# Output projection: from weights stationary, one pair of output tiles at a time, to token tiles stationary and weights 512 columns wide

## The chip, the cores and the metric

The kernel runs on one core of a Trainium2 chip. TensorE (PE) multiplies 128 x 128 stationary tiles with a moving operand of up to 512 columns into PSUM; VectorE (DVE) and ScalarE (ACT) do the elementwise work; DMA transfers are issued from the queues of SyncE (SP), ACT and GpSimd (POOL). GpSimd's DMAs can add to what is in the destination. The metric is the device time of one execution in microseconds; lower is better.

## The reference, cut to what matters

One layer of a streaming encoder, 512 tokens of width 2048, in float32. The normed input goes through one projection to queries, keys, values and gates of three token mixers with four heads each, and to merge gates. Each mixer's result is gated, projected up to 2048, weighted by its merge gate, and summed. The last line is what the change is about.

```python
hn = rmsnorm(x, norm_g)
proj = jnp.einsum('bsd,dc->bsc', hn, w_in)
...
up = jnp.einsum('bsnw,nwd->bsnd', ys, w_up)
merged = jnp.sum(gates * up, axis=2)
return x + jnp.einsum('bsd,de->bse', merged, w_out)
```

## The kernel before

Numbers are split into a high part in the float32r format, which PE reads in one pass, and a low part, the difference. A product is three matmuls: high by high, high by low, low by high. ACT makes the high part of a weight tile (`split`, line 249), DVE the low part (line 253).

The projections use seven block products in place of eight (Strassen's scheme in Winograd's form). The blocks are the two halves of the input dimension, two weight tiles or two blocks of weight columns, and the two halves of the tokens, 256 each. On the data's side the combinations are made once. For the output projection these are `m1` (products 1 and 5), `m2` (2 and 3), `m23` (6 and 7) and `m4` (4), one for each of eight pairs of merged tiles (`merged_a`, `merged_b`, from line 1672). On the weights' side they are made for each task: w5 = a21 + a22 and w7 = a11 + a21 by DMAs of GpSimd that add onto a tile just loaded (`add_up`, line 291), w6 = w1 + w5 and w3 = w2 + w6 by DVE (`sums`, lines 658 and 664).

A `PairTask` (line 614) makes two tiles of 128 output columns for all tokens, as seven units of one product each. A unit has a weight tile of eight 128 x 128 blocks, which are stationary; the data move. For each block j, a matmul of 512 columns takes the high and low parts of the data side by side, and a matmul of 256 columns takes the low weights with the high data. The two halves of the PSUM bank are added on the way out (`fold`). Products 6, 7, 4 and 3 go on in the bank of 1, 6, 7 and 5 (`ONTO`).

The stages, in order on PE: the columns of the input projection with the three mixers' attention between them, until 1008 us; the up projection, 16 tiles of two units each; the output projection, `out_pair(e)` for eight pairs of output tiles (line 1723). Its first pair is `late`: its order is 1, 5, 2, 3, 6, 7, 4, its banks are not shared, and it uses 256-wide matmuls only, three for each block. The last product of the last pair has 256-wide matmuls too (`plain_end`). Outputs are 128 output columns on partitions by 512 tokens; x is loaded as xT and added by DVE (lines 1738, 1746 and 1753), and stores go out on ACT's queue (lines 1740, 1747 and 1755).

The order of the instructions is written by a planner when the program is built. Every stretch of work is a generator that yields an engine and a cost, an event, or slots of a buffer. `Flow.run` always takes the task that can start first, and among several the one that is due first. So the orders on PE, ACT, DVE and SP's DMAs are fixed in the program, and each engine waits only for the data of its next instruction. GpSimd has no clock in the plan. An `add_up` of a pair task is not pinned in the order, while those of the value tasks (`pinned=True`, line 945) are; the transfer time is counted at 170 KB per us behind the load, in the order in which loads are listed.

Buffers: six raw weight tiles of 512 KB (`NR`), three split ones (`LA` + 1), 20 tiles of 256 KB (`NT`), 28 split data tiles (`NX`), eight PSUM banks (two of `acc0`, one each of `acc1` and `acc2`, four of `att`). A unit is prepared from the start of the unit two places ahead of it.

`ValueTask` (line 885) is the one place that already has data stationary and weights moving: two token blocks take turns with 256 weight columns.

Of the kernel before, what the change touches and what calls it, by code (L numbers as in the profile page):

```python
# [9 lines left out]
F32R = mybir.dt.float32r  # L10
# [6 lines left out]
P = 128  # L17
HP = P // 2
S = 512
# [18 lines left out]
PE, ACT, DVE, SP = 0, 1, 2, 3  # L38
# [26 lines left out]
class Flow:  # L65
# [98 lines left out]
def hybrid_kernel(  # L164
# [126 lines left out]
    def add_up(to, src, ready, kb, pinned=False):  # L291
        i = nc.gpsimd.dma_start(to, src, accum_op=ALU.add)  # L292
# [91 lines left out]
    def load_unit(u):  # L384
        if isinstance(u, (Pair, VUnit)):
            if u is u.task.units[0]:
                yield from u.task.load()
            return
# [203 lines left out]
    class Pair(Unit):  # L592


        def __init__(self, task, i):
            super().__init__(task.mms_of(i), task.after_of(i))
            self.task, self.p = task, task.order[i]
            self.single = task.late or task.plain_end and self.p == 4
            self.onto = None if task.late else ONTO.get(self.p)
            self.turns, self.opens = not self.single, self.onto is None  # L600
# [13 lines left out]
    class PairTask:  # L614
# [9 lines left out]
        def __init__(self, src1, src2, ops, c1_done=None, c2r_done=None, c2_done=None, late=False, rest=None,  # L624
                     x1_first=False, plain_end=False):
            self.plain_end = plain_end
            self.src, self.ops, self.late, self.rest = (*src1, *src2), ops, late, rest
            self.done = {"c1": c1_done, "c2r": c2r_done, "c2": c2_done}
            self.order = (1, 5, 2, 3, 6, 7, 4) if late else (1, 2, 6, 5, 7, 3, 4)
# [4 lines left out]
            self.r, self.r_ev, self.c2_ev, self.right_ev = None, Event(), Event(), Event()  # L634
# [38 lines left out]
        def mms_of(self, i):  # L673
            p = self.order[i]
            bank = (0, 1, 2, 0, 0, 1, 2)[i] if self.late else {2: 1, 5: 2, 3: 2}.get(p, 0)
            self.bank[p] = bank

            def go(u):
                single, onto = u.single, u.onto
# [8 lines left out]
                def high(first):  # L688
                    for j in range(UK):
# [4 lines left out]
                        if single:  # L694
                            yield PE, mm_us(HS)
                            mm(self.ps[p][:, LH], u.hi[:, j, :], r[:, 0, :], start, stop, more)
                            yield PE, mm_us(HS)
                            mm(self.ps[p][:, LH], u.hi[:, j, :], r[:, 1, :], more=more)
                        else:
                            yield PE, mm_us(S)  # L700
                            mm(two(self.ps[p]), u.hi[:, j, :], r, start, stop, more)
# [16 lines left out]
        def after_of(self, i):  # L718
# [20 lines left out]
            def late():  # L739
                ps, bank = self.ps[p][:, LH], accs[self.bank[p]]  # L740
                if p == 1:
                    yield from new("u")
                    yield ACT, act_us(HS)
                    nc.scalar.activation(self.u[:, LH], ps, AF.Copy)
                elif p == 5:
                    yield from new("c2")
                    yield ACT, act_us(HS)
                    nc.scalar.activation(self.c2[:, RH], ps, AF.Copy)
                elif p == 2:
                    yield from new("c1")  # L750
                    yield ev[1]
                    yield h
                    add(self.c1[:, LH], self.u[:, LH], ps)
                elif p == 3:
                    yield ev[2]
                    yield ev[5]
                    yield h
                    add(self.c1[:, RH], self.c2[:, RH], ps)
                elif p == 6:
                    yield ev[2]  # L760
                    yield h
                    add(self.u[:, LH], self.u[:, LH], ps)
                elif p == 7:
                    yield ev[6]
                    yield h
                    add(self.u[:, RH], self.u[:, LH], ps)
                else:
                    yield ev[7]
                    yield h
                    minus(self.c2[:, LH], self.u[:, RH], ps)  # L770
                give(bank)
                set_(ev[p])
                if p == 6:
                    yield ev[3]
                    yield h
                    add(self.c1[:, RH], self.c1[:, RH], self.u[:, LH])
                    finished("c1", self.c1)
                elif p == 7:
                    yield ev[3]
                    yield h  # L780
                    minus(self.c2[:, RH], self.c2[:, RH], self.u[:, RH])
                    finished("c2r", self.c2[:, RH])
                elif p == 4:
                    give(t2s)
# [1123 lines left out]
```

## Time and profile before

| what | value |
|---|---|
| median of 3 runs | 1298.85 us (1298.83 to 1299.65) |
| the profiled execution | 1298.3 us |
| its span, first to last instruction | 1296.5 us |
| PE busy | 1289.8 us, 99% |
| DVE busy | 1148.6 us, 89% |
| ACT busy | 884.3 us, 68% |
| GpSimd busy | 106.9 us, 8% |
| first to last matmul of the output projection | 1135.6 to 1293.2 us |
| granted PE clock | 1.000 |

Times inside the span are counted from its first instruction. A row of a group reads: line, engine, operation, output <- inputs, shapes, count, then busy us and mean ns of one, then the engine's idle time ahead of these instructions and what ended it. The ends of matmuls are modelled, and a matmul's duration overlaps the next one's, so that the distance from one start to the next tells the pace. PEld stands for the loads of stationary tiles. A row of a timeline reads: start, length, engine, line, operation, tiles, shape, count.

### The profile page before, as it was taken

The numbers are of one execution on the slowest core, as the hardware profiler recorded it, in microseconds if no ns is written. First come the engines' busy times: TensorE is split into PE (matmuls) and PEld (weight loads), VectorE is DVE, ScalarE is ACT, GpSimd is POOL, SyncE is SP. The second block draws the span as 40 slices with busy tenths as digits, with TensorE's granted clock in tenths as the row PEclk, the third lists the DMA queues.
The fourth block names the chain that finished last, engine by engine and source line by source line (L and its number), as shares of the span: only waits on it lengthen the run. The fifth ranks groups of instructions, "written<-read, shape, count | busy, mean of one in ns | idle before, by whom it ended". The sixth has DMA issues, their size and how long they took to land.

```text
span 1296.5 us, 20194 instructions
## 1 busy us (share of the span) xinstructions
PE 1289.8 (99%) x7247; PEld 1127.6 (87%) x7247; DVE 1148.6 (89%) x1693; ACT 884.3 (68%) x1380; POOL 106.9 (8%) x138
## 2 busy tenths in 40 slices
PE   9999999999999999999999999999999999999998
PEld 6888888888888888888888888888888888898887
DVE  8988889888998999989799999999899888898776
ACT  8887677777767668676766785967858555454443
POOL 0200001020110000102010000100000000001000
PEclk9999999999999999999999999999999999999999
DMA  9879798888889778888897888888988755778893
GB/s 341 236 189 234 195 239 195 216 197 230 223 198 251 181 209 207 243 207 232 209 237 202 191 230 220 200 241 188 234 222 273 240 191 188 204 206 244 233 255 97
DMA packets 132420, 282.90 MB, mean 218 GB/s; under 512 B 43344, under 2 KB 51536, under 8 KB 132320
## 3 DMA queue, kind: packets, MB, share of 16 engines
q1 hardware_dynamic: 111200, 217.32, 54.0%
q0 software_dynamic: 17376, 59.78, 27.2%
q10 hardware_dynamic: 3744, 4.52, 1.0%
q8 instruction: 57, 0.93, 0.3%
q14 instruction: 43, 0.35, 0.1%
HBM read 249.92 MB, written 24.42 MB: 212 GB/s over the span
## 4 chain that ended last, share of the span: by engine, by line
PE 92%; DVE 4%; DMA 1%; issue 1%; ACT 1%; SPq 1%; DVEq 0%; ACTq 0%
PE acc L268 77%; PE att L268 10%; DVE w L253 2%; PE att L1386 1%; PE att L1387 1%; PE att L264 1%; PE att L265 1%; SPq L281 1%; PE att L263 1%; PE att L1385 1%; DVE m L253 0%; DMA tt<-p 0%; DMA lf_parts<-fd 0%; DMA gl<-c 0%; DVE c L538 0%
## 5 line engine op out<-in xcount | busy, mean ns | idle before, releaser
L253 DVE TENSOR_TENSOR w<-raw,w 128x1024 fp32r<-128x1024 f32 (+2 forms) x424 | 500.3, 1185 | 96.2 <-ACT w L249 95.4
L249 ACT ACTIVATE w<-raw 128x1024 fp32r<-128x1024 f32 (+2 forms) x424 | 434.7, 1026 | 173.1 <-PE acc L268 78.6
L268 PE MATMUL acc<-x,w 128*128 128x512 f32 (+1 forms) x2656 | 497.2, 339 | 0.7 <-ACT w L408 0.7
L268 PEld LDWEIGHTS acc<-x,w 128*128 128x128 f32 x2656 | 426.0, 189 | 66.5 <-issue 2.5
L268 PE MATMUL acc<-t,w 128*128 128x512 f32 (+1 forms) x1920 | 358.7, 338 | 0.4 <-DVE w L253 0.3
L268 PEld LDWEIGHTS acc<-t,w 128*128 128x128 f32 x1920 | 291.5, 190 | 33.3 <-ACT vh L249 0.4
L268 PE MATMUL acc<-m,w 128*128 128x256 f32 (+1 forms) x960 | 157.3, 327 | 0.3 <-DVE m L253 0.3
L268 PEld LDWEIGHTS acc<-m,w 128*128 128x128 f32 x960 | 141.4, 190 | 16.3 <-DVE m L253 0.5
L292 POOL DMA_DIRECT2D raw<-in_w_col x80 | 69.0, 863 | 776.2 <-DMA raw<-in_w_col 298.8
L268 PE MATMUL att<-y,w 128*128 128x512 f32 x384 | 89.6, 389 | 0.0
L268 PEld LDWEIGHTS att<-y,w 128*128 128x128 f32 x384 | 72.1, 188 | 14.9
L268 PE MATMUL acc<-w,x 128*128 128x512 f32 (+1 forms) x336 | 63.8, 339 | 0.0
L818 ACT ACTIVATE u<-acc 128x512 f32<-128x512 f32 x49 | 29.1, 594 | 46.5 <-PE acc L268 44.2
L797 ACT ACTIVATE u<-acc 128x512 f32<-128x512 f32 x50 | 29.7, 594 | 43.3 <-PE acc L268 35.0
L658 DVE TENSOR_TENSOR raw<-raw,raw 128x1024 f32<-128x1024 f32 x48 | 58.6, 1221 | 0.3
L664 DVE TENSOR_TENSOR raw<-raw,raw 128x1024 f32<-128x1024 f32 x48 | 58.6, 1220 | 0.2
L268 PEld LDWEIGHTS acc<-w,x 128*128 128x128 f32 x336 | 52.2, 190 | 7.1 <-issue 0.4
L538 DVE TENSOR_TENSOR c<-c,begin_in 128x512 f32<-128x512 f32 x80 | 54.3, 686 | 0.2
L852 ACT ACTIVATE c<-acc 128x256 f32<-128x256 f32 x49 | 18.7, 381 | 49.7 <-PE acc L268 41.9
L801 ACT ACTIVATE v<-acc 128x512 f32<-128x512 f32 x53 | 31.5, 594 | 28.3 <-PE acc L268 28.1
L737 DVE TENSOR_TENSOR c<-u 128x256 f32<-128x256 f32 x105 | 44.3, 425 | 3.2
L268 PE MATMUL acc<-y,w 128*128 128x512 f32 x192 | 46.1, 389 | 0.0
(216 smaller groups left out, 1359.6 us busy)
## 6 DMA issues: line engine op xcount, KB each, us to landing
raw<-in_w_col SPq DMA_DIRECT2D x200, 512.0 KB, 4.9
raw<-in_w_col POOLq DMA_DIRECT2D x80, 512.0 KB, 6.7
raw<-in_w_out SPq DMA_DIRECT2D x40, 512.0 KB, 4.3
raw<-in_w_v SPq DMA_DIRECT2D x24, 512.0 KB, 5.4
gl<-c SPq DMA_DIRECT2D x48, 256.0 KB, 3.9
raw<-in_w_up SPq DMA_DIRECT2D x32, 384.0 KB, 3.8
sg<-gl SPq DMA_DIRECT2D x48, 256.0 KB, 3.9
raw<-in_w_out POOLq DMA_DIRECT2D x16, 512.0 KB, 7.3
```

The lines of the kernel that those rows point to most:

```text
L249: nc.scalar.activation(hi, src, AF.Copy)
L253: nc.vector.tensor_sub(lo, src, f(hi))
L268: nc.tensor.matmul(ps, w, x, start=start, stop=stop, skip_group_check=more)
L292: i = nc.gpsimd.dma_start(to, src, accum_op=ALU.add)
L538: nc.vector.tensor_mul(c, c if src is None else src, rstd[0][:c.shape[0], :])
L658: nc.vector.tensor_add(w[1], w[1], w[5])
L664: nc.vector.tensor_add(w[2], w[2], w[1])
L737: add(to, src[:, LH], src[:, RH])
L797: nc.scalar.activation(self.u, ps, AF.Copy)
L801: nc.scalar.activation(self.v, ps, AF.Copy)
L818: nc.scalar.activation(self.s, ps, AF.Copy)
L852: nc.scalar.activation(c, ps[:, RH], AF.Copy, scale=-1.0)
```

## The change

The output projection is written anew. `OutTask` g (two of them) makes 1024 output columns as two blocks of 512; tokens are on partitions. A unit `OutUnit` is one product p on a quarter kq of its input dimension: two input blocks (`QK`) of 512 weight columns. For each of the two 128-token blocks s of a product, the token tile is stationary and 512 weight columns move: high by high, low data by high weights, and, once the low weights are there, high data by low weights. That is 12 matmuls of 512 in a unit, 28 units in a task. All three parts add up in the same columns, so there is no fold. The units of products 1 and 5 come first, those of 4 last; the last unit of all cuts its second token block into two halves of 256 columns.

Results go by DVE straight from PSUM onto tiles that hold x, loaded by rows of tokens from `xn` (`begin`, `result`), and the tiles are stored from SP's queue, the last half one from ACT's. Product 7's weight is w6 less a22, subtracted by DVE (`seventh`), in place of a load and an add on GpSimd; product 4's weight comes in 256 KB tiles. The split of `m4` moves from the up projection (`merged_b`) to a task that waits for the end of the up projection (`merged_d`), and it takes data tiles in place of 256 KB tiles. The late first pair, `plain_end` and what belongs to them are removed.

In the whole kernel GpSimd becomes an engine of the planner (`POOL`): an `add_up` waits in the plan until its load has landed (`added`), takes 0.8 us of GpSimd and is pinned in the order; its transfer counts at 190 KB per us. The first loads of a value task's product 7, which are issued by GpSimd too, are listed in the same way, and the extra 1 us on the value task's sums (`VLATE`) goes. The input `w_out` and the output are laid out to match.

```diff
...
-PE, ACT, DVE, SP = 0, 1, 2, 3
+PE, ACT, DVE, SP, POOL = 0, 1, 2, 3, 4
...
-    LATE = (0.3, 0.12, 0.12, 0.0)
+    LATE = (0.3, 0.12, 0.12, 0.0, 0.0)
 
     def __init__(self):
-        self.clock = [0.0] * 4
-        self.idle = [0.0] * 4
+        self.clock = [0.0] * 5
+        self.idle = [0.0] * 5
...
-    def add_up(to, src, ready, kb, pinned=False):
-        i = nc.gpsimd.dma_start(to, src, accum_op=ALU.add)
-        if pinned:
-            tc.keep_in_program_order(i)
-        line[0] = max(line[0], ready + 1.0) + kb / 170.0
+    def add_up(to, src, kb):
+        yield POOL, 0.8
+        tc.keep_in_program_order(nc.gpsimd.dma_start(to, src, accum_op=ALU.add))
+        line[0] = max(line[0], flow.fin + 1.0) + kb / 190.0
         return Event(line[0] + 2.5)
+
+    def added(there, begun, parts):
+
+        yield begun
+        for to, src, kb in parts:
+            ev = yield from add_up(to, src, kb)
+        there.t = ev.t
...
                 ev = yield from fetch(t, srcs[0], 512)
                 if len(srcs) > 1:
-                    ev = add_up(t, srcs[1], ev.t, 512)
-                self.there[p].t = ev.t
+                    spawn(added(self.there[p], ev, [(t, srcs[1], 512)]), 0.0, flow.fin)
+                else:
...
                 for to, c in pieces(p, kh):
                     w, kb = src({5: 2, 1: 0, 2: 1, 7: 0, 4: 3}[p], kh)[:, c], 128 * (c.stop - c.start)
-                    if queue is nc.sync:
+                    if p == 7:
+                        yield POOL, 0.8
+                        tc.keep_in_program_order(nc.gpsimd.dma_start(to, w))
+                        ev = Event(landing(flow.fin, kb))
+                    else:
                         ev = yield from fetch(to, w, kb)
-                    else:
-                        tc.keep_in_program_order(queue.dma_start(to, w))
-                        ev = Event(landing(flow.ready + 0.5, kb))
+                if p in (5, 7):
+                    more = [(to, src({5: 3, 7: 2}[p], kh)[:, c], 128 * (c.stop - c.start)) for to, c in pieces(p, kh)]
+                    return lambda: spawn(added(self.there[p, kh], ev, more), 0.0, flow.fin)
...
                 if p == 5:
-                    add(p, kh)
+                    add()
+            adds = []
             for kh in range(2):
-                yield from begin(7, kh, nc.gpsimd)
+                adds.append((yield from begin(7, kh)))
+            for add in adds:
+                add()
             for kh in range(2):
-                add(7, kh)
-            for kh in range(2):
-                yield from begin(4, kh, nc.sync)
+                yield from begin(4, kh)
...
-        yield t2s, 1
-        parts, ev = t2("m4", F32R), Event()
-        yield from split(parts[:, LH], parts[:, RH], b[:, RH], HS, ev)
-        give(t2s)
-        m4[k] = two(parts), parts[:, LH], ev
+        spawn(merged_d(k, b), 6.0, flow.fin)
...
-    mops = strassen_ops(m1, m2, m23, None)
-    mops[4] = lambda k: m4[k]
...
-    def out_pair(e):
...
+    mops = strassen_ops(m1, m2, m23, m4)
+
+    def merged_d(k, b):
+
+        yield up_done
+        for i in range(UK):
+            yield lambda: m23[i] is not None
+        if k % 2 == 0:
+            yield xps, 1
+            m4[k // 2] = Parts("m4")
+        yield lambda: m4[k // 2] is not None
+        h, lo, ev = m4[k // 2].half(k % 2)
+        yield from split(h, lo, b[:, RH], HS, ev, (up_done.t + 10.0 + k,))
+        give(t2s)
...
+    QK = UK // 4
...
+    class OutUnit(Unit):
+
+
+        def __init__(self, task, p, kq):
+            super().__init__(task.mms, None, (QK, S))
+            self.task, self.p, self.kq = task, p, kq
...
+        def __init__(self, g, last):
+            self.g, self.last = g, last
+            order = [(p, q) for q in range(4) for p in (1, 5)]
+            order += [(6, 0), (2, 0), (6, 1), (3, 0), (2, 1), (6, 2), (3, 1), (2, 2), (6, 3), (3, 2), (2, 3)]
+            order += [(7, q) for q in range(4)] + [(3, 3)] + [(4, q) for q in range(4)]
+            self.w, self.there = {}, {o: Event() for o in order}
+            self.units = [OutUnit(self, *o) for o in order]
...
+        def load(self):
+            def src(i, kq):
+                return w_out[self.g, i // 2, i % 2, kq]
+
+            def begin(p, kq):
+                yield raws, 1
+                t = raw_tile((QK, S))
+                self.w[p, kq] = [t]
+                ev = yield from fetch(t, src({1: 0, 5: 2, 2: 1}[p], kq), 512)
+                if p == 5:
+                    spawn(added(self.there[p, kq], ev, [(t, src(3, kq), 512)]), 0.0, flow.fin)
+                else:
+                    self.there[p, kq].t = ev.t
+
+            def pairs():
+                for kq in range(4):
+                    yield t2s, QK
+                    self.w[4, kq] = [t2("raw").rearrange("p (j c) -> p j c", j=1) for _ in range(QK)]
+                    for j, t in enumerate(self.w[4, kq]):
+                        ev = yield from fetch(t, src(3, kq)[:, j:j + 1], 256)
+                    self.there[4, kq].t = ev.t
+
+            for o in ((5, 0), (1, 0), (5, 1), (1, 1), (5, 2), (5, 3), (1, 2), (1, 3)):
+                yield from begin(*o)
+            for kq in range(4):
+                if kq == 1:
+                    spawn(pairs(), 0.5, flow.fin)
+                yield from begin(2, kq)
...
+        def sums(self):
+            n = dve_us(QK * S)
+            for kq in range(4):
+                yield self.there[1, kq]
+                yield self.there[5, kq]
+                yield self.unit(1, kq).ready
+                yield DVE, n, flow.ready + 4.0
+                a = self.w[1, kq][0]
+                nc.vector.tensor_add(a, a, self.w[5, kq][0])
+                self.w[6, kq] = [a]
+                set_(self.there[6, kq])
+                spawn(self.free(5, kq), 1.0)
+            for kq in range(4):
+                yield self.there[2, kq]
+                yield self.unit(2, kq).ready
+                yield DVE, n, flow.ready + 1.0
+                self.w[3, kq] = [a] = self.w[2, kq]
+                nc.vector.tensor_add(a, a, self.w[6, kq][0])
+                set_(self.there[3, kq])
+                spawn(self.seventh(kq), 1.0)
+
+        def seventh(self, kq):
+            yield self.unit(6, kq).ready
+            yield self.there[4, kq]
+            self.w[7, kq] = [a] = self.w[6, kq]
+            for j, t in enumerate(self.w[4, kq]):
+                yield DVE, dve_us(S), flow.ready + 6.0
+                nc.vector.tensor_sub(a[:, j:j + 1], a[:, j:j + 1], t)
+            set_(self.there[7, kq])
+
+        def free(self, p, kq):
+
+            yield self.unit(p, kq).ready
+            give(raws)
...
+        def begin(self):
+            for i in (1, 4, 2, 3):
+                for s in range(2):
+                    yield t2s, 1
+                    b, c = (s, 2 + s, s, 2 + s)[i - 1], 2 * self.g + (i > 2)
+                    t = self.o[i, s] = t2("o")
+                    self.o_ev[i, s].t = (yield from fetch(t, xn[b, c], 256)).t
...
+        def mms(self, u):
+            p, kq = u.p, u.kq
+            onto = ONTO.get(p)
+            ends = self.last and p == 4 and kq == 3
...
+            def step(s, part, cols):
+                for j in range(QK):
+                    k = kq * QK + j
+                    yield lambda: mops[p](k) is not None
+                    r, _, ev = mops[p](k)
+                    yield ev
+                    yield PE, mm_us(cols.stop - cols.start)
+                    w = u.lo if part == 1 else u.hi
+                    mm(self.ps[p, s][:, cols], r[:, part // 2, s * P:(s + 1) * P], w[:, j, cols],
+                       onto is None and kq + j + part == 0, kq == 3 and j == QK - 1 and part == 1, True)
+
+            whole = slice(0, S)
+            if ends:
+                yield u.ready
+                for s, cols in ((0, whole), (1, LH), (1, RH)):
+                    yield from bank(s)
+                    for part in (0, 2, 1):
+                        yield from step(s, part, cols)
+                    spawn(self.result(p, s, cols), 0.0, flow.fin)
+                return
+            for s in range(2):
+                yield from bank(s)
+                for part in (0, 2):
+                    yield from step(s, part, whole)
+            yield u.ready
+            for s in range(2):
+                yield from step(s, 1, whole)
+                if kq == 3:
+                    spawn(self.result(p, s, whole), 0.5, flow.fin)
+
+        def result(self, p, s, cols):
+            ps = self.ps[p, s][:, cols]
+            add, sub = nc.vector.tensor_add, nc.vector.tensor_sub
+            first = {1: (1, add), 5: (4, sub), 6: (2, add), 4: (3, sub)}.get(p)
+            then = {2: (1, add, 1), 3: (2, add, 6), 7: (4, sub, 5)}.get(p)
+            i, do = (first or then)[:2]
+            if first:
+                yield self.o_ev[i, s]
+            else:
+                yield self.ev[then[2], s]
+            o = self.o[i, s][:, cols]
+            yield DVE, dve_us(cols.stop - cols.start)
+            do(o, o, ps)
+            if p not in (1, 5, 6, 7) and cols.stop == S:
+                if s:
+                    give(atts)
+                else:
+                    give(accs[{2: 1, 3: 2, 4: 0}[p]])
+            if cols.stop == S:
+                set_(self.ev[p, s])
+            if p in (2, 3, 7, 4):
+                b, c = (s, 2 + s, s, 2 + s)[i - 1], 2 * self.g + (i > 2)
+                if cols.start:
+                    nc.scalar.dma_start(out[b, c][:, cols], o)
+                else:
+                    t2s.free.append((yield from store(out[b, c][:, cols], o, 256)))
+
+    for g in range(2):
+        units.extend(OutTask(g, g == 1).units)
...
-VLATE = 1.0
...
-_OUT = (DT, P, S)
+_OUT = (QB, NQ, P, S)
...
-        "w_out": g["w_out"][0].reshape(2, UK, P, DT, P).transpose(3, 0, 2, 1, 4),
+        "w_out": g["w_out"][0].reshape(2, 4, 2, P, 2, 2, S).transpose(4, 5, 0, 1, 3, 2, 6),
...
-    return np.ascontiguousarray(o.reshape(D, S).T).reshape(1, S, D)
+    return np.ascontiguousarray(o.reshape(QB, NQ, P, S).transpose(0, 2, 1, 3)).reshape(1, S, D)
...
```

More of the change, by code (lines that the diff above doesn't have):

```diff
@@ L597, in __init__ @@
             self.task, self.p = task, task.order[i]
-            self.single = task.late or task.plain_end and self.p == 4
-            self.onto = None if task.late else ONTO.get(self.p)
-            self.turns, self.opens = not self.single, self.onto is None
+            self.onto = ONTO.get(self.p)
+            self.turns, self.opens = True, self.onto is None
         def source_there(self):
@@ L674, in mms_of @@
             p = self.order[i]
-            bank = (0, 1, 2, 0, 0, 1, 2)[i] if self.late else {2: 1, 5: 2, 3: 2}.get(p, 0)
+            bank = {2: 1, 5: 2, 3: 2}.get(p, 0)
             self.bank[p] = bank
             def go(u):
-                single, onto = u.single, u.onto
+                onto = u.onto
                 more = onto is not None
@@ L737, in fold @@
                     add(to, src[:, LH], src[:, RH])
[L739 to L783, printed above, removed]
-                    give(t2s)
-                    finished("c2", self.c2)
-            def go():
-                if i == 0 and self.rest is not None:
-                    spawn(self.rest(self), 1.0)
-                if self.late:
-                    yield from late()
-                    return
+            def go():
                 ps, bank = self.ps[p], self.pools[self.bank[p]]
@@ L1763, in hybrid_kernel @@
-    for e in range(0, DT, 2):
-        units.extend(out_pair(e))
+    mops = strassen_ops(m1, m2, m23, m4)
[10 more added lines that the diff above has]
+        give(t2s)
```

121 lines of the change are left out of this document (48 added, 73 removed).

## The prediction

> **What bounds the kernel now.** I read the page first: the engines' shares and the chain that ended last.
>
> ```profile
> PE 1289.8 (99%) x7247; PEld 1127.6 (87%) x7247; DVE 1148.6 (89%) x1693; ACT 884.3 (68%) x1380; POOL 106.9 (8%) x138
> ...
> PE 92%; DVE 4%; DMA 1%; issue 1%; ACT 1%; SPq 1%; DVEq 0%; ACTq 0%
> ```
>
> TensorE (PE) is busy for 99% of the span and carries 92% of the chain. VectorE (DVE) is next at 89%, close enough to become the bound wherever the change loads it. Next, busy time by stretches of the span (columns: stretch, its length, then busy time and instructions of PE, weight loads, DVE, ScalarE and GpSimd, the granted clock, DMA share, GB/s):
>
> ```profile
> 0.00:300.00 300.00, 297.36 (x1648) 254.80 (x1649) 266.80 (x419) 230.71 (x410) 32.13 (x50) 1.00 0.85 226
> 300.00:600.00 300.00, 300.00 (x1729) 265.39 (x1728) 272.66 (x387) 217.92 (x330) 28.11 (x34) 1.00 0.86 217
> 600.00:900.00 300.00, 300.00 (x1732) 265.62 (x1731) 276.94 (x413) 217.13 (x333) 25.92 (x31) 1.00 0.86 216
> 900.00:1008.00 108.00, 107.57 (x621) 94.92 (x620) 97.94 (x145) 77.59 (x121) 6.91 (x8) 1.00 0.91 237
> 1138.00:1155.00 17.00, 16.68 (x139) 16.41 (x138) 16.86 (x27) 8.10 (x13) 0.87 (x1) 1.00 0.48 136
> 1155.00:1280.00 125.00, 125.00 (x723) 110.50 (x722) 99.35 (x124) 59.09 (x71) 10.36 (x12) 1.00 0.85 238
> ```
>
> The clock is full everywhere. Before 1008 us PE idles 2.64 + 0 + 0 + 0.43 = 3.1 us, so a better order can win almost nothing there, and a worse one can lose. The output projection (from 1135.6 us) is PE's too, except that in its first part DVE is busy for 16.86 of 17.00 us. What counts in that stage is how long PE's stream of matmuls takes. A matmul's own duration is modelled and overlaps the next, so I take strides: stretches divided by counts. The chain by time gives the up projection, all matmuls 512 wide; the PE timeline gives a value unit, which already holds token tiles stationary while weights move:
>
> ```profile
> 1007.91 5.44 PE att L268 x24
> ```
>
> ```profile
> 603.41 1.07 PE L268 MATMUL acc<-w,t 128*128 128x512 f32 x4
> ...
> 605.23 0.64 PE L268 MATMUL acc<-w,t 128*128 128x256 f32 x4
> ...
> 607.14 1.09 PE L268 MATMUL acc<-w,t 128*128 128x512 f32 x4
> 608.07 1.07 PE L268 MATMUL att<-w,t 128*128 128x512 f32 x4
> 608.98 0.39 PE L268 MATMUL acc<-w,x 128*128 128x512 f32 x1
> ```
>
> 24 in 5.44 us is 0.2267 us for a 512-wide matmul. In the value unit eight take 605.23 - 603.41 = 1.82 us (0.2275 each) and sixteen 256-wide ones 607.14 - 605.23 = 1.91 us (0.119). The next eight 512-wide ones take 608.98 - 607.14 = 1.84 us (0.230): long ones right after short ones are slower. Now the output projection itself, its groups by shape, then PE's busy time in two stretches:
>
> ```profile
> L268 PEld LDWEIGHTS acc<-m,w 128*128 128x128 f32 x960 | 141.4, 190 | 16.3 <-DVE m L253 0.5
> ...
> L268 PE MATMUL acc<-m,w 128*128 128x512 f32 x384 | 92.8, 391 | 0.0
> ...
> L268 PE MATMUL acc<-m,w 128*128 128x256 f32 x576 | 74.3, 283 | 0.3 <-DVE m L253 0.3
> ```
>
> ```profile
> 1135.60:1293.20 157.60, 157.26 (x961) 1.00 0.75 209
> 1160.00:1280.00 120.00, 120.00 (x691) 1.00 0.85 237
> ```
>
> Between 1160 and 1280 us the widths alternate eight by eight or sixteen by sixteen, half of each, so 691 matmuls in 120 us make 0.3473 us for one of each, and a 256-wide one costs 0.3473 - 0.2267 = 0.1206 us. At equal columns two short ones cost 2 x 0.1206 - 0.2267 = 0.0145 us more than a long one. The count closes: 384 x 0.2267 + 576 x 0.1206 = 156.5 us of the stage's 157.60; the other 1.1 us are 0.32 us of idle (the row 1138 to 1155), the drain of the last matmul and the slower long ones.
>
> **The change part by part.**
>
> *Matmuls.* Columns stay: 384 x 512 + 576 x 256 = 344,064 before, and 56 units of 12 x 512, also 344,064, after. The count falls from 960 to 672, or 678 with six of the last unit cut in two: 666 x 0.2267 + 12 x 0.1206 = 152.4 us, with 0.15 us of drain 152.6, against 157.6 us: **-5.0 us**, all on the path. The other end takes the value unit's slow stride for all: 666 x 0.230 + 1.45 + 0.15 = 154.8 us, so -2.8 us. I take -5.0, because the slow stride stands behind short matmuls, and the new stream has none before its last unit. The stationary load must stay hidden: 190 ns, one for every matmul as before, now under a stride of 227 ns instead of partly 121.
>
> The Trainium skill, "TensorE: Matmul & The Clock Gate", section "Back-to-back issue gap", speaks against this term: it gives N/2.4 + 2.5 ns for the gap, a fixed 2.5 ns per matmul, by which 282 fewer matmuls bring only 0.7 us and the stage would not pay. The rows disagree (0.2267 and 0.1206 us lie 13 to 14 ns above N/2.4), and the sum goes by the rows.
>
> *Changeover from the up projection.* Before, products 1 and 5 cover 48 x 0.1206 = 5.8 us, then product 2 needs the last merged tile. After, products 1 and 5 cover 96 x 0.2267 = 21.8 us with m1 alone. Prices on DVE (groups after 1149 us), and ScalarE's (ACT) split:
>
> ```profile
> L253 DVE TENSOR_TENSOR w<-raw,w 128x1024 fp32r<-128x1024 f32 x51 | 62.1, 1223 | 25.6 <-ACT w L249 25.6
> L664 DVE TENSOR_TENSOR raw<-raw,raw 128x1024 f32<-128x1024 f32 x7 | 8.5, 1221 | 0.0
> ...
> L822 DVE TENSOR_TENSOR v<-v,acc 128x512 f32<-128x512 f32 x7 | 4.8, 687 | 0.0
> ...
> L1746 DVE TENSOR_TENSOR c<-c,xr 128x256 f32<-128x256 f32 x8 | 3.4, 421 | 0.1
> ```
>
> ```profile
> L249 ACT ACTIVATE w<-raw 128x1024 fp32r<-128x1024 f32 x49 | 51.7, 1056 | 32.4 <-PE acc L268 16.9 <-DVE c L1746 3.4 <-DVE w L253 3.0
> ```
>
> DVE in one group of 28 units: 28 low parts x 1.22 = 34.2 us, 8 weight sums x 1.22 = 9.8, 8 subtractions for product 7 x 0.69 = 5.5, 14 results x 0.69 = 9.7. That is 59.2 us beside 336 x 0.2267 = 76.2 us of PE, or 78% (before: 99.35 of 125, 79%). The folds, ACT's copies out of PSUM and the separate additions of x go; they lay beside PE, so nothing is gained. But the first group also gets the rest of the merging: 8 x 0.69 for m23, 8 x 0.42 for m4 (moved here from the up projection), and some 4 us for the last tile by my estimate from the same rows. That is 72 us of 76, 95%. A unit's low part is used only after eight of its twelve matmuls, 1.8 us in, and its split is begun two units ahead, so lateness of a few us is covered. I charge +0.5 us, near the 0.32 us that PE idles today with DVE at 99%; the ends are 0 and 4 us (the room that is left).
>
> *Loads and stores.* Per group 12 plain tiles, 4 added onto and 8 halves: 10 MB, 20 MB in all, against 56 x 0.5 = 28 MB.
>
> ```profile
> raw<-in_w_out SPq DMA_DIRECT2D x40, 512.0 KB, 4.3
> ...
> raw<-in_w_out POOLq DMA_DIRECT2D x16, 512.0 KB, 7.3
> ```
>
> The tightest tile is (1, 2), the seventh for six buffers: it waits until (5, 0) is summed, and PE needs it 4 x 2.72 = 10.9 us into the stage. With 4.3 us to land and 1.06 us to split, the sum must be done 5.5 us in; I expect it by 3. If that cover goes, PE waits for the difference. Stores of results move from ACT's queue to SP's, where the tile loads behind them wait for the result too; those loads run some five units (13.6 us) ahead, which hides a late result of 0.69 us. GpSimd's 8 adds instead of 16, and 16 loads of x as before, lie beside PE as well: nothing.
>
> *The end.* The last part is subtracted and stored as before:
>
> ```profile
> 1293.23 0.42 DVE L849 TENSOR_TENSOR c<-c,acc 128x256 f32<-128x256 f32 x1 [1.00 <-PE acc L268]
> 1293.68 0.34 ACTq L1755 DMA_DIRECT2D out<-c  x1
> ```
>
> That store ends the span 2.8 us after its issue. After, 512 KB instead of 384 KB leave in the last 1.5 us; 128 KB at the 237 GB/s above are 0.5 us. I take +0.3 us between 0 and 0.5.
>
> *GpSimd (POOL) in the list.* All its DMAs get a written order and count as 0.8 us of an engine; weight sums fall due at other planned times, so the written orders of DVE and ACT shift everywhere. Is anyone waiting for adds today (columns: total us, times, longest)?
>
> ```profile
> POOL raw L292 <- DMA raw<-in_w_col: 298.8, 29, 16.4
> ...
> ACT w L249 <- DMA raw<-in_w_col: 1.7, 1, 1.7
> ```
>
> POOL waits 298.8 us for the loads that it adds to, while ACT waits for such tiles once, 1.7 us: they lie ready early, which covers the order of the adds. I take 0. The ends are -1 us (the 0.43 us of idle from 900 us on, and as much from the 2.64) and +8.5 us, below.
>
> **Sum.** -5.0 + 0.5 + 0.3 + 0 = -4.2 us. The profiled execution took 1298.3 us, so 1294.1; the median of the runs, 1298.85, lies 0.55 us above it, so 1294.6 us.
>
> **The rivals.**
>
> *DVE holds the first group.* At 95% the written order breaks somewhere, for instance at (1, 2): 3 to 4 us of PE idle in place of 0.5, so 1294.6 + 3 = 1297.6 us, no change. For it: DVE at 16.86 of 17.00 today. Against: that stretch loses only 0.32 us, and products 1 and 5 now cover four times as much.
>
> *Fewer matmuls don't pay.* Then the change doesn't do what it says: with each long matmul behind a new stationary tile at 157.6 / 672 = 0.2345 us the time is as before, 1298.9 us. For it: the 0.230 above points that way. Against: 0.2275 in the same unit, each matmul there with another token tile. The Trainium skill's gap, named above, would put the time there too; no row bears it out.
>
> *A written POOL order stalls PE upstream (slower).* An add queued behind one whose tile is late comes late by one landing, 7.3 us in the row above; with a lead of two units (16 x 0.3473 = 5.6 us) PE loses 1.7 us each time. Three such places eat the gain, five among the 40 column pairs make 1294.6 + 8.5 = 1303.1 us. For it: PE has no idle to give between 300 and 900 us, and DVE stands at 272.66 and 276.94 of 300 in an order written anew. Against: ACT hardly waits for tiles.
>
> *The new order also closes gaps.* The changeover costs nothing and 1 us goes upstream: 1294.6 - 0.5 - 1 = 1293.1 us.
>
> **How the numbers follow.** Forecast 0.58, closed gaps 0.10, DVE in the first group 0.12, fewer matmuls for nothing 0.05, POOL 0.15. About 0.2% (2.6 us) is what a measurement can tell from no change, so the bounds are 1296.25 and 1301.45 us: faster 0.58 + 0.10 = 0.68, same 0.12 + 0.05 = 0.17, slower 0.15. The range leaves out the POOL rival: from 1291.3 (closed gaps, an end that costs nothing and 1.5 us more upstream) to 1299.5 us (matmuls for nothing, 0.6 us of stall beside them). The forecast alone, with its bounds, spans 1293.5 to 1297.
>
> **What would show it.** PE's timeline of the output projection should have 678 matmuls in about 153 us, nearly all 512 wide, 227 ns apart. A stage of 158 us without idle says matmuls for nothing; idle behind w or raw in its first 76 us says DVE or loads; PE idle well above 3.1 us before 1008 us says the written order. The prediction is wrong if the long stride is not 227 ns there, or if PE gains over 2 us of idle anywhere.

## The result and the profile after

The changed kernel takes 1296.26 us (median of 14 runs, 1294.24 to 1299.18) against 1299.5 us (14 runs, 1297.39 to 1300.3): 3.2 us less, a ratio of 0.9978 with a 95% interval of 0.9971 to 0.9986. The profiled execution took 1295.77 us, its span 1294.0. From its page, the engines' shares and the chain:

```profile
PE 1286.2 (99%) x6965; PEld 1112.3 (86%) x6965; DVE 1137.9 (88%) x1666; ACT 873.4 (68%) x1359; POOL 100.0 (8%) x130
...
PE 93%; DVE 3%; DMA 2%; ACT 1%; SPq 1%; issue 1%; ACTq 0%; DVEq 0%
```

PE still carries the time, with 282 matmuls fewer. Now the same stretches as in the prediction (busy time of PE, weight loads, DVE, ScalarE and GpSimd, then clock, DMA share and GB/s), and the output projection's matmuls by shape with PE's busy time from its first matmul to its last:

```profile
0.00:300.00 300.00, 298.01 (x1652) 255.26 (x1653) 266.39 (x420) 233.44 (x413) 32.22 (x50) 1.00 0.84 225
300.00:600.00 300.00, 300.00 (x1731) 265.29 (x1730) 272.58 (x388) 219.11 (x332) 29.88 (x36) 1.00 0.86 219
600.00:900.00 300.00, 298.67 (x1722) 264.06 (x1721) 274.16 (x409) 212.94 (x325) 24.11 (x28) 1.00 0.84 214
900.00:1008.00 108.00, 107.40 (x618) 94.24 (x617) 98.95 (x146) 77.14 (x120) 6.90 (x8) 1.00 0.90 236
1138.00:1155.00 17.00, 17.00 (x77) 14.08 (x76) 16.93 (x26) 11.14 (x18) 0.00 (x0) 1.00 0.56 186
1155.00:1280.00 125.00, 125.00 (x553) 103.47 (x552) 98.01 (x111) 49.27 (x53) 3.45 (x4) 1.00 0.52 159
```

```profile
L268 PE MATMUL acc<-w,m 128*128 128x512 f32 x336 | 94.2, 389 | 0.0
L268 PE MATMUL att<-w,m 128*128 128x512 f32 x330 | 92.6, 389 | 0.0
L268 PE MATMUL att<-w,m 128*128 128x256 f32 x12 | 1.9, 290 | 0.5 <-DVE o L1846 0.5
```

```profile
1137.30:1290.60 153.30, 152.78 (x679) 1.00 0.50 156
1160.00:1280.00 120.00, 120.00 (x531) 1.00 0.50 153
```

Three things are to be seen. The stage has 678 matmuls, 226 ns apart (120 us for 531), and lasts 153.4 us instead of 157.6. It begins at 1137.3 us instead of 1135.6, mostly because PE stood for 1.3 us between 600 and 900 us, where it stood for nothing before. And near the end PE waits once, 0.5 us, for DVE. The spans differ by 2.5 us: -4.2 from the stage and +1.7 ahead of it, while what follows the last matmul is as long as before (3.3 us).

The loss upstream, on ACT and on PE, and the wait near the end:

```profile
657.99 0.63 ACT L249 ACTIVATE vh<-vr 128x512 fp32r<-128x512 f32 x1 [3.38 <-DMA vr<-vd]
658.53 0.58 ACT L742 ACTIVATE u<-acc 128x512 f32<-128x512 f32 x1
659.16 1.20 PE L268 MATMUL acc<-t,w 128*128 128x512 f32 x4 [1.33 <-ACT u L742]
```

```profile
1289.54 0.42 DVE L1846 TENSOR_TENSOR o<-o,att 128x256 f32<-128x256 f32 x1 [0.38 <-PE att L268]
1290.02 0.62 PE L268 MATMUL att<-w,m 128*128 128x256 f32 x3 [0.52 <-DVE o L1846]
```

ACT stands 3.38 us for `vr`, the value tiles read back from DRAM for a head's attention. Behind it stands the copy `u`, which frees the PSUM bank in which PE's next product goes on. Near the end, PE writes the right half of a bank only when DVE has read its left half.

### The profile page after: what moved, and what is told of

It reads as the page before. It is cut to its first block, busy times and chain, and to the rows that moved or that the text cites. A ratio compares the mean times of both kernels' runs of the same rounds, so it can differ in the third digit from the quotient of the medians.

```text
span 1294.0 us, 19495 instructions
## 1 busy us (share of the span) xinstructions
PE 1286.2 (99%) x6965; PEld 1112.3 (86%) x6965; DVE 1137.9 (88%) x1666; ACT 873.4 (68%) x1359; POOL 100.0 (8%) x130
## 4 chain that ended last, share of the span: by engine, by line
PE 93%; DVE 3%; DMA 2%; ACT 1%; SPq 1%; issue 1%; ACTq 0%; DVEq 0%
PE acc L268 72%; PE att L268 17%; DVE w L253 1%; SPq L281 1%; DMA vr<-vd 1%; PE att L264 1%; PE att L265 1%; PE att L263 1%; PE att L1321 1%; PE att L1322 1%; PE att L1320 0%; DMA lf_parts<-fd 0%; ACT w L249 0%; DMA tt<-p 0%; DMA raw<-in_w_one 0%
## 5 line engine op out<-in xcount | busy, mean ns | idle before, releaser
L268 PE MATMUL att<-w,m 128*128 128x512 f32 (+1 forms) x342 | 94.5, 386 | 0.5 <-DVE o L1846 0.5
L268 PE MATMUL acc<-w,m 128*128 128x512 f32 x336 | 94.2, 389 | 0.0
L268 PEld LDWEIGHTS att<-w,m 128*128 128x128 f32 x342 | 63.6, 188 | 13.7 <-DVE o L1846 0.7
L268 PEld LDWEIGHTS acc<-w,m 128*128 128x128 f32 x336 | 63.1, 188 | 13.2
L662 DVE TENSOR_TENSOR raw<-raw,raw 128x1024 f32<-128x1024 f32 x40 | 48.8, 1220 | 0.4
L668 DVE TENSOR_TENSOR raw<-raw,raw 128x1024 f32<-128x1024 f32 x40 | 48.7, 1218 | 0.2
L742 ACT ACTIVATE u<-acc 128x512 f32<-128x512 f32 x43 | 25.5, 594 | 33.4 <-PE acc L268 33.2
L1548 ACT ACTIVATE sg<-sg,small_in 128x512 f32<-128x512 f32 x48 | 33.4, 715 | 21.4 <-DMA sg<-gl 21.4
L763 ACT ACTIVATE u<-acc 128x512 f32<-128x512 f32 x42 | 24.9, 592 | 33.0 <-PE acc L268 30.7
```

Of the source, the lines that this page charges most:

```text
L268: nc.tensor.matmul(ps, w, x, start=start, stop=stop, skip_group_check=more)
L662: nc.vector.tensor_add(w[1], w[1], w[5])
L668: nc.vector.tensor_add(w[2], w[2], w[1])
L742: nc.scalar.activation(self.u, ps, AF.Copy)
L763: nc.scalar.activation(self.s, ps, AF.Copy)
L1548: nc.scalar.activation(g, g, AF.Sigmoid, bias=bg[:, n * DT + d:n * DT + d + 1])
```

## The experiments

My theory was the prediction's: the count of matmuls carries the gain, and the changeover, the end and the list of GpSimd's queue cost what was put down. The rivals were that the list stalls PE, that DVE binds the changeover, and that the count is not what pays. Below, what PE "lost" at a place is the distance from one matmul's start to the next, less the usual stride; that is about 0.16 us more than the wait that a row shows. Ratios are to the kernel before as it ran beside each experiment.

**The two parts apart.** First the new output projection without the list:

```diff
-    def add_up(to, src, kb):
-        yield POOL, 0.8
-        tc.keep_in_program_order(nc.gpsimd.dma_start(to, src, accum_op=ALU.add))
-        line[0] = max(line[0], flow.fin + 1.0) + kb / 190.0
+    def add_up(to, src, ready, kb, pinned=False):
+        i = nc.gpsimd.dma_start(to, src, accum_op=ALU.add)
...
+        line[0] = max(line[0], ready + 1.0) + kb / 170.0
```

> The new output projection alone; GpSimd's adds are as in the kernel before (not in the plan, counted at 170 KB per us behind their load). Theory: the gain is the projection's stream of matmuls and the list costs about 1.5 us upstream (GpSimd listed, weight loads are planned closer together, the reload of the value tiles, vr from vd, lands late, and ACT with the copy that frees a PSUM bank stands behind it). Then the projection starts near 1135.6 us as before, lasts 153 to 153.5 us, ACT waits for vr by under 1 us in total, and the time is 4.2 us under the kernel before, ratio 0.9968. Rival: the stall upstream comes from any replanning, the list is innocent: start near 1137 and ratio 0.998 as the changed kernel.

Measured: 1297.75 us against 1299.18, ratio 0.9990 (0.9982 to 0.9999). The projection starts at 1136.0 us, so less is lost upstream, but it lasts 155.7 us: PE loses 2.26 us in the changeover. ACT's waits for `vr` are 3.2 us in three places, where the theory had under 1. PE's waits, the largest (total, times, longest):

```profile
PE acc L268 <- DVE w L253: 2.8, 3, 2.1
```

Neither theory had this. Then the list alone, by the same lines put into the kernel before:

> The kernel before with GpSimd in the plan alone, the old output projection. Theory: ACT's waits for vr grow to some 6 us as in the changed kernel, PE stalls by 1 to 2 us before 1008 us, and the time is 1 to 1.7 us over the kernel before, ratio 1.001. Rival (list innocent): ratio 1.000 within 0.0005 and no PE wait over 0.7 us between 100 and 900 us. A third: the list gains, ratio under 0.9995.

Measured: 1299.92 us, ratio 1.0004 (0.9995 to 1.0013). ACT's waits for `vr` did grow, from 0.6 us in one place to

```profile
ACT vh L249 <- DMA vr<-vd: 7.2, 5, 2.4
```

but PE lost only 0.21 us at 658 us and started the projection at 1135.8. So the list has no price of its own that this can show. How much of the waits for `vr` it brings is not shown either: they were 3.2 us without it, above, and 2.7 to 7.5 us in six executions of the changed kernel's order (below). They reach PE only when the landing is late enough.

**The late `vr`.** One edit planned every landing of `vr` later, a second one only that of the eighth head, the one at 657 us (with the interleaved end, below):

```diff
-            yield ev
+            yield Event(ev.t + 3.0)
...
-            yield ev
+            yield Event(ev.t + (3.0 if (self.n, self.h) == (B, 3) else 0.0))
```

> The changed kernel with the landing of vr planned 3 us later, all else the same, so that ACT takes other work first. Theory (late vr is the stall at 657 us): ACT's waits for vr go from 6.9 us to under 2, PE's wait of 1.3 us for ACT's copy at 657 us goes, the time is about 1.4 us under the changed kernel (ratio to before near 0.9967) and the runs scatter less than its 5 us. Rival: the stall only moves to another place or was of that one execution: ratio 0.998 and the same scatter.

Measured: 1297.65 us, ratio 0.9993 (0.9984 to 1.0002), no faster than without the edit. ACT's waits for `vr` fell to 0.2 us and the stall at 657 us went, as the theory had it. But the whole order was planned anew, and PE now lost 1.12 us at 264 us and 1.06 us in the changeover, and the scatter stayed (1296.28 to 1300.19). The cause was right and the remedy wrong: here the stall that was planned away was replaced by others.

> As the run with the interleaved end, and one landing of vr alone, that of the eighth head (649 us), planned 3 us later, which moves its attention work behind the next product and leaves the rest of the order as it is. Theory (ACT stands at this late vr with the copy that frees PE's bank behind it): PE's stall at 657 us, 1.5 and 2.3 us in two executions of the same order, goes, nothing else moves, and the time is 1.5 to 2 us under the interleaved end alone: ratio near 0.9960, and the scatter of runs shrinks. Rival (a stall follows from the DMA load there and takes the next waiting instruction): the time is as with the interleaved end alone.

Measured: 1294.57 us, ratio 0.9969 (0.9959 to 0.9978). Only 29 places of PE's order differ from the changed kernel's, 12 of them in the last unit. PE is busy for 300.00 of 300.00 us between 600 and 900 us, and the projection starts at 1135.1. The run with the later `m4` (below) has the same order there and loses nothing at 657 us either. The place is settled by that, but the time lies within the interval of the interleaved end alone, so what it is worth on average was not shown.

**The end.** First the last unit in one piece, then its three pieces in another order:

```diff
-                for s, cols in ((0, whole), (1, LH), (1, RH)):
+                for s, cols in ((0, whole), (1, whole)):
...
+                for s, cols in ((1, LH), (0, whole), (1, RH)):
```

> The changed kernel with the second token block of the very last unit in one piece of 512 columns, not two of 256. Theory: the 0.67 us in which PE waits for DVE's read of the left half before it writes the right half of the same bank goes, and six matmuls fewer save 0.09 us; the last subtraction is 0.27 us longer (0.69 for 0.42) and the last store has 256 KB instead of 128 KB (0 to 0.4 us): 0.1 to 0.5 us faster than the changed kernel. Rival: PE's wait has another cause and stays: 0.2 to 0.6 us slower than it.

Measured: 1296.37 us, ratio 0.9982 (0.9973 to 0.9991), as the changed kernel. PE's wait near the end is gone, but what follows the last matmul grew from 3.32 to 3.93 us, so both sides cancel. Up to that unit the order is the changed kernel's, so this is also a second execution of it: at 657 us PE lost 2.34 us, with 1.6 us more behind it at a lower clock (last section), and 0.53 us in the changeover.

> The changed kernel with the last unit in another order: left half of the second token block, then the whole first block, then the right half. The order of all other work is unchanged. Theory (PE waits for DVE's read of the left half before it writes the right half of the same bank): the read hides behind the first block's 1.36 us, PE's wait of 0.5 us near the end goes, the stage from its first to its last matmul is 0.67 us shorter than the changed kernel's, and the end after it stays 3.3 us: ratio 0.0005 under that of the changed kernel. Rival: the wait stands for something else and stays.

Measured: 1295.11 us, ratio 0.9966 (0.9954 to 0.9978). DVE reads the left half while PE works on the other block, the wait is gone, and 0.2 us of it come back after the last matmul (3.52 us). Without what was lost in the changeover the stage is 0.67 us shorter, as expected. The time is not clearly under the changed kernel's: the intervals of the ratios overlap. In this third execution of the order PE lost 0.62 us at 657 us and 0.95 in the changeover.

**Is it the count?** Every long matmul of the stage was cut into two on the same stationary tile:

```diff
-                    mm(self.ps[p, s][:, cols], r[:, part // 2, s * P:(s + 1) * P], w[:, j, cols],
+                    for c in ((LH, RH) if cols == whole else (cols,)):
+                        mm(self.ps[p, s][:, c], r[:, part // 2, s * P:(s + 1) * P], w[:, j, c],
```

> The changed kernel with every 512-wide matmul of the new output projection cut into two of 256 columns onto the same stationary tile: the same columns, 1344 matmuls. Theory (a matmul costs 13 to 14 ns beside its columns, so the count carries the gain): 120 ns each, the stage grows from 153.4 to about 161.5 us, 8 us more. Rival (the cost per matmul is about 2.5 ns, and the gain came from elsewhere, such as the late first pair or fewer evictions): 672 x 2.5 ns, the stage grows by 1.7 us to about 155.

The sums come out otherwise than the reference's, perhaps because both halves that open a bank carry its start flag, which was not tested; the matmuls are all there. Measured: one run of 1306.90 us. PE's busy time in the stage:

```profile
1139.60:1301.80 162.20, 161.67 (x1345) 1.00 0.48 149
```

At equal columns 666 more matmuls cost 162.2 - 153.4 = 8.8 us, 13 ns each. Both stages hold the same 0.67 us near the end and lose nothing in the changeover. The theory holds, and the rival's 1.7 us is excluded. Each half also loads its stationary tile anew (1344 loads in the stage), so the 13 ns belong to a matmul with its load; which of the two makes them stays open. The run's order up to the projection is the changed kernel's once more: it lost 1.73 us at the late `vr`, 1.52 at 115 us, and started the projection at 1139.6 us.

**Who binds the changeover?** Eight more DVE operations of 0.69 us in the first 22 us:

```diff
+            def more():
+                yield DVE, dve_us(S), flow.ready + 0.5
+                nc.vector.tensor_add(x_begin, x_begin, x_begin)
+
+            if self.g == 0 and p in (1, 5):
+                spawn(more(), 0.5, flow.fin)
```

> The changed kernel with one more 512-wide addition on DVE (0.69 us, on a tile that nothing reads any more) in each of the first group's eight units of products 1 and 5: 5.5 us more for DVE in the first 22 us of the output projection, where it is busy for 10.63 of 10.70 and 12.00 of 12.00 us. Theory of the prediction (a few us of lateness are covered): PE loses under 1.5 us there. Rival (DVE is already the bound there, the cover is used up): PE loses 3 to 5.5 us in that stretch.

Measured: one run of 1300.99 us. PE's busy time in three stretches (the column after the count is the granted clock):

```profile
1137.00:1149.00 12.00, 12.00 (x54) 1.00 0.57 184
1149.00:1161.00 12.00, 7.61 (x29) 0.94 0.47 146
1161.00:1163.00 2.00, 2.00 (x6) 0.51 1.02 290
```

PE lost 2.42 and 2.30 us, 4.7 in all: the rival holds. Up to the second wait six of the eight additions had run, 3.6 us at their pace of 0.60 us. The runs of the same order whose projection starts as early (1135.8 and 1135.3 us, here 1135.9) lost 0.95 and 1.35 us without them, so 3.4 to 3.8 us are due to the additions: next to nothing was covered. DVE is the bound of the changeover. This is also why a stall upstream and the wait here don't simply add: in the changed kernel's profile DVE ends the low part that PE waits for at 1155.2 us and in the other two at 1154.8 to 1154.9, while PE starts the stage 1.4 to 1.9 us later in the first and so loses nothing.

What does DVE do there? Its timeline in the run with the interleaved end, up to the row for which PE waits, and PE's:

```profile
1151.49 1.22 DVE L1751 TENSOR_TENSOR raw<-raw,raw 128x1024 f32<-128x1024 f32 x1
1152.62 1.09 DVE L253 TENSOR_TENSOR m<-sg,m 128x256 fp32r<-128x256 f32 x3
1153.63 1.22 DVE L253 TENSOR_TENSOR w<-raw,w 128x1024 fp32r<-128x1024 f32 x1
```

```profile
1154.90 0.73 PE L268 MATMUL acc<-w,m 128*128 128x512 f32 x2 [0.79 <-DVE w L253]
```

The three rows of 256 columns are splits of `m4`, which no matmul reads for about another 48 us (product 4 begins 24 units, 65 us, into the stage); the low part that PE waits for stands behind them. So they were made due later, in two kernels: the one with one later `vr` and the interleaved end, and the new projection without the list.

```diff
-        yield from split(h, lo, b[:, RH], HS, ev, (up_done.t + 10.0 + k,))
+        yield from split(h, lo, b[:, RH], HS, ev, (up_done.t + 28.0 + k,))
```

> As the run with one vr later and the interleaved end, and the splits of m4, which product 4 needs only 65 us into the output projection, due 18 us later in the plan; all before the projection keeps its order. In the runs before, these eight splits (0.42 us each, 3.4 us of DVE) stand in the first 20 us of the projection, where DVE has no gap, ahead of the low parts of weights that PE waits for. Theory (DVE is the bound of the changeover, and m4 needn't be there): PE's wait for DVE there, 0.8 us in the run with one vr later, goes to under 0.3, the stage lasts 152.6 to 152.9 us, the time falls by 0.5 to 0.9 us to near 1294. Rival (the wait is the late landing of the eighth tile, for which ACT stands 3 us): the wait stays near 0.8.

Measured: 1293.59 us, ratio 0.9963 (0.9950 to 0.9975). ACT still waits for landings, 2.8 us for the eighth tile and 3.2 for the next one, PE hardly; the waits of both, the largest on PE in the stage and ACT's for tiles:

```profile
PE acc L268 <- DVE o L1846: 0.2, 1, 0.2
```

```profile
ACT w L249 <- DMA raw<-in_w_out: 6.0, 2, 3.2
```

The time is not clearly under that of the run it builds on (0.9969, 0.9959 to 0.9978).

> The new projection alone (GpSimd not in the plan, the end not interleaved) with the same later m4. There PE waited 2.26 us in the changeover for a low part behind DVE's other work. Theory (DVE's order): the wait falls under 0.7 us, the ratio goes from 0.9990 to about 0.9975, and so most of the list's apparent worth was the order of the changeover. Rival (late landing, or the list itself): the wait stays over 1.5 us and the ratio at 0.999.

Measured: 1295.05 us, ratio 0.9970 (0.9959 to 0.9981), which does not overlap with the 0.9982 to 0.9999 of the same kernel with the early `m4`. What PE lost in the changeover fell from 2.26 to 0.32 us. The two rows, early `m4` first:

```profile
1150.98 0.72 PE L268 MATMUL acc<-w,m 128*128 128x512 f32 x2 [2.10 <-DVE w L253]
```

```profile
1149.44 0.74 PE L268 MATMUL acc<-w,m 128*128 128x512 f32 x2 [0.16 <-DVE w L253]
```

The orders of PE, ACT, GpSimd and SP are the same in both, instruction for instruction; 26 places of DVE's differ. A late landing is no rival for this stall: ACT had split that weight tile by 1146.6 us, and its first wait for a tile of this stage, 2.4 us, ends at 1158.4. So DVE's order made the stall, and the list's apparent worth with it: without the list, and with `m4` out of the way, the new projection is as fast as the changed kernel.

> The changed kernel as it is, on the same chip as the two others. Its order is fixed, so the stall at 657 us shows how far it varies with the landing of vr: 1.5 and 2.3 us (the run with the last unit whole has the same order there) and 0.6 us (the run with the interleaved end) so far. Expected: between 0.3 and 2.5 us, a changeover wait of 0 to 1 us, and a ratio of 0.9975 to 0.9982, above the run with the later m4 by 0.001.

Measured: 1295.82 us, ratio 0.9977 (0.9968 to 0.9986). In this execution of the order PE lost 0.29 us at 657 us and 1.35 us in the changeover, the first at the edge of what was expected, the second beyond it; the projection started at 1135.3 us.

The version with the later `m4`, the one later `vr` and the interleaved end is the fastest that was run: 2.2 us under the changed kernel beside it, though the intervals of their ratios still overlap.

## Why the prediction was right, and where it wasn't

The forecast was -4.2 us and 1294.6 us; measured were -3.2 us and 1296.26 us. The difference is off by 1.0 us and the time by 1.7, because the kernel before came out at 1299.5 us, not at the 1298.85 from which the forecast started. The direction and the range hold. By its steps:

*Matmuls, -5.0 us.* Right, and for the reason given. The stage went from 157.60 to 153.38 us, and of the latter 0.67 us are the wait near the end: 4.9 us on the stream. The stride is 226 ns with other stationary tiles throughout, and the run with the matmuls cut in two puts 13 ns on each. The rule of the Trainium skill that stood against the term ("TensorE: Matmul & The Clock Gate", section "Back-to-back issue gap") does not hold for these matmuls: 2.5 ns beside the columns would have made 1.7 us of the 8.8. The section itself gives that formula for an isolated matmul, not for a stream of loads and matmuls, so the prediction leaned on it for more than it says.

*Changeover, +0.5 us.* The size was right by luck of the mean, one argument for it wrong. Four executions of the same order lost 0, 0.53, 0.95 and 1.35 us, 0.7 on average. The prediction held that lateness of a few us is covered by the later use of the low part; 3.6 us more work on DVE cost PE 3.4 to 3.8 us. It also counted `m4`'s splits over the whole first group, 76 us, while the plan puts them into its first 20. The rival "DVE holds the first group" named the mechanism, and in the new projection without the list it took 2.26 us; in the changed kernel's own profile it cost nothing, where PE came 1.4 us later than in the run with the interleaved end.

*Loads.* The tile (1, 2) was called the tightest, and it came in time. It is ACT that waits for the last tile of products 1 and 5, 2.1 us in the profile and up to 3.5 in other runs; with `m4` out of the way PE hardly felt it.

*The end, +0.3 us.* The term was put in the wrong place. More bytes at the end cost nothing (3.36 us before, 3.32 after the last matmul); what cost 0.67 us was PE's wait between the halves of one bank, which the prediction did not see in the cut of the last unit.

*GpSimd in the list, 0.* Right for the list by itself, 1.0004 with an interval over 1. But the sum had no term for what any new order does to a PE without slack. In six executions with the new order up to there (the last two are the runs with halves and with more DVE work) the projection started at 1137.3, 1138.9, 1135.8, 1135.3, 1139.6 and 1135.9 us, against 1135.6 in the one profile of before. That is 1.5 us on average. The late `vr` cost 0.3 to 2.3 us of it, once with 1.6 us of lower clock behind it; in the run with halves other waits cost as much. With the 0.67 us at the end this is enough for the miss, but it is no exact sum: single executions of the changed kernel lie between 1294.24 and 1299.18 us. The slower rival had the wrong mechanism: in the changed kernel's profile ACT waits for no tile of the column pairs, so no add held up another where it matters; a transfer that the plan expects too early stood ahead of a copy on ACT. By the prediction's own sign of being wrong, over 2 us of idle gained anywhere, the profile after passes, but the run with the last unit whole, the same order up to there, stood 2.18 us at that place: the assumption that the order costs nothing upstream was the weak one.

*Matmuls for nothing* is excluded. *The new order also closes gaps* did not happen in the changed kernel.

## What to carry to other kernels

Where TensorE is busy all the time, count its instructions: at equal columns every matmul less, with its load, saved 13 ns here, and that part of the sum came out within 0.1 us. Any change of the order then moves single stalls of one or two microseconds about, so give the sum a term for that, and compare several executions of one order before a stall is explained. And look in a full changeover for work that is due only much later: moving 3.4 us of it out of the way took 1.9 us of waiting from TensorE where it hit.

## What the hardware showed that I had not expected

After PE had stood twice for a little over 2 us, 2.9 us apart, its granted clock fell to 0.51 (the row 1161 to 1163 of the run with more DVE work). In the run with the last unit whole a single wait of 2.2 us was enough (the column after the count is the granted clock):

```profile
655.00:670.00 15.00, 12.82 (x66) 0.89 0.83 221
```

Eight matmuls after that wait were 200 ns longer each, 1.6 us on top of the stall. The length of the wait does not decide it alone: the 1.3 us of the changed kernel's profile had no such tail, but neither had the 2.1 us of the new projection without the list, nor the first of the two waits above (2.25 us). What else decides was not tested. The Trainium skill, "TensorE: Matmul & The Clock Gate", section "What's actually happening", names an idle window of some 3.4 us for the fall to half; here it came after less.
